# Squares of a norm kept in fp32 and added in pairs, so that half as many sum matmuls follow, in an 8-core decoder trunk

## The chip, the cores and the metric

The kernel runs on all 8 cores of one Trainium2 chip, with the same program on every core and no exchange between them. Each core works on one prompt of 2048 tokens and on 16 decode rows. The metric is the device time of the slowest core in microseconds (us).

An execution of this program can fall into a slower state: the cores of one die (0 to 3, or 4 to 7) show a lower granted TensorE clock and take some per cent longer. Only fast executions are compared here, and traces are read on cores at the full clock (about 0.98).

Names used: PE is TensorE, DVE is VectorE, ACT is ScalarE, POOL is GpSimd, SP is SyncE (which issues the stores). L700 is line 700 of the kernel; the same line has another number in every edited kernel.

## The reference, cut to what matters

```python
D_MODEL = 1024; DEPTH = 4; RMS_EPS = 1e-6

def _rmsnorm(x, g):
    xf = x.astype(jnp.float32)
    y = xf * lax.rsqrt(jnp.mean(xf * xf, axis=-1, keepdims=True) + RMS_EPS)
    return (y * g.astype(jnp.float32)).astype(x.dtype)

def _layer(x, ...):
    h = _rmsnorm(x, norm1_g)
    z = h @ w_in
    # ... gated conv branch, S5 state space branch, gated merge m ...
    x = x + m @ w_out
    h2 = _rmsnorm(x, norm2_g)
    gate, up = jnp.split(h2 @ w_gate_up, [D_FF], axis=-1)
    x = x + (jax.nn.silu(gate) * up) @ w_down
    return x, ...
# four layers, then a last _rmsnorm(x, final_g)
```

## The kernel before

The sequence is treated in two halves of 1024 tokens. The first half carries the decode rows too and is cut into three blocks of 384, 384 and 272 columns; the second has two blocks of 512. Channels lie on partitions, so the 1024 channels are eight tiles per block, and the mean over channels is a sum over partitions. A matmul with a matrix of ones makes that sum.

```python
    PP = Pool("psum", 8, lambda s: PSUM[s], reserve=3)
    SP_ = Pool("sc", NSC - 4, lambda s: SC[:, s, :], reserve=2)       # 5 shared scratch slots
    SQ = Pool("sq", 4, lambda s: SC[:, NSC - 4 + s, :], reserve=-1)   # 4 slots for the layer's parameter tables
    ...
    def norm(half, blk, l, which, src=None):
        xin = src or (lambda kt: (X[:, kt, blk.c0:blk.c0 + n], xkeys(kt, blk)))
        ps = PP.new()
        n = blk.n
        hq = lambda kt: (R if which == "fg" else H)[:, kt, blk.c0:blk.c0 + n]
        qkeys = rkeys if which == "fg" else hkeys
        for kt in range(8):
            act(lambda e, kt=kt: e.activation(out=hq(kt), in_=xin(kt)[0], func=AF.Square),
                xin(kt)[1], qkeys(kt, blk), n)
            S.pe([(lambda e, kt=kt: e.matmul(ps[:, 0:n], lhsT=ONESB[:], rhs=hq(kt), start=(kt == 0), stop=(kt == 7)),
                   qkeys(kt, blk) + [C_("ONESB")], MMN(n))], [(ps,)], FULL)
        rs = SP_.new()
        # ... Ln and Exp on ACT: rs = (mean + eps) ** -0.5 ...
        for kt in range(8):
            if which == "fg":      # the final norm
                o = SP_.new()
                # ... o = x * g * rs on DVE, then a store of o by SP ...
            else:
                # ... H[:, kt] = x * g * rs on DVE (scalar_tensor_tensor) ...
```

- The squares are bf16 and lie in H, exactly where the normalised values go afterwards. They need no slot of their own. Only the final norm ("fg") puts them into R.
- The five shared scratch slots also hold rs, the outputs of SiLU and sigmoid, and the output tiles of the final norm until their stores have landed. Four other slots belong to the layer's parameter tables. Those tables are worked out only in the first half, on DVE and POOL, and stay for the second.
- Nothing is ordered at run time. A list scheduler with its own cost model (the lines `MMN`, `ACT_`, `tt` give durations) fixes the order on every engine when the program is built, and each engine then runs its list strictly in order.

There are 45 norms per program: 27 in the first half and 18 in the second. Three of the 27, the three blocks' first norm of layer 0, are called "the start" below. The final norm of the first half and the first norm of the second half, which meet, are called "the turn".

## Time and profile before

The median is 3668.1 us over four fast executions (3666.34 to 3668.78).

| what | value | read from |
|---|---|---|
| PE busy | 3527.6 of 3684.6 us, 96% | page, busy times (core 1, the slowest in the profile) |
| DVE, ACT, POOL busy | 46%, 31%, 12% | page, busy times |
| chain of work that ended last | 91% PE | page, chain |
| PE idle before sum matmuls into H (L700) | 25.1 us | page, costliest groups |

The first fence is from the page of the kernel before: the span, the busy times, the chain by engine, and three of the costliest groups. A group line gives line, engine, operation, output<-inputs and count, then after the first bar the busy time (us) and the mean (ns) of one, then after the second bar the idle time of that engine just before these instructions and what ended most of it.

```profile
span 3684.6 us, 66888 instructions; the slowest of 8 cores (3655.5 to 3684.6 us)
PE 3527.6 (96%) x23912; PEld 1987.8 (54%) x23912; DVE 1699.6 (46%) x3049; ACT 1134.0 (31%) x2144; POOL 439.7 (12%) x639
PE 91%; DVE 3%; issue 3%; DMA 1%; ACT 1%; SPq 1%; DVEq 0%; ACTq 0%
...
L654 POOL DMA_DIRECT2D RING<-wpk x472 | 251.6, 534 | 2920.8 <-PE ps L667 2678.0
L722 DVE SCALAR_TENSOR_TENSOR H<-X,PRM,SC 128x384 bf16<-128x384 f32 (+2 forms) x304 | 190.9, 698 | 35.1 <-ACT SC L705 34.9
...
L700 PE MATMUL ps<-H,ONESB 128*128 128x384 bf16 (+2 forms) x320 | 77.6, 349 | 25.1 <-ACT H L698 25.1
```

PE is the bound. POOL spends little on arithmetic, and mostly waits for PE to free a weight slot (L654). The 320 sums into H have 25.1 us of PE idle in front of them in the whole program, nearly all of it at the start (the same view of core 6, cut to the first 262 us, has 23.5).

The second fence is from the list of cores, kernel before. Die 0 ran at a slightly lower clock in this execution, so the traces of die 1 are read.

```profile
die 0 (median of its cores): 3674.2 us, clock 0.975
die 1 (median of its cores): 3659.6 us, clock 0.981
```

The third is from the timeline of the start, kernel before, core 6. Its columns are start (us), time from first to last instruction of the row (us), engine, line, operation, count, and in brackets the idle time before it with what ended it.

```profile
30.08 2.67 ACT L698 ACTIVATE H<-X 128x272 bf16<-128x272 f32 x8 [0.27 <-DMA X<-xsT]
30.66 2.62 PE L700 MATMUL ps<-H,ONESB 128*128 128x272 bf16 x8 [2.23 <-ACT H L698]
...
32.64 12.37 DVE L722 SCALAR_TENSOR_TENSOR H<-X,PRM,SC 128x384 bf16<-128x384 f32 x15
...
33.38 0.49 ACT L703 ACTIVATE SC<-ps,CST 128x272 f32<-128x272 f32 x1 [0.63 <-PE ps L700]
```

The third block's eight squares take 2.67 us in one run, its sums follow within 0.6 us, and Ln starts at 33.38 us.

### The profile page before, as it was taken

The page shows a single profiled execution, that of the slowest core. Times are in us where ns is not written, and L with a number is a line of the kernel's source. Part 1 is how long each engine was busy: PE and PEld are TensorE (multiplying, and loading weights), DVE is VectorE, ACT ScalarE, POOL GpSimd, SP SyncE. Part 2 cuts the span into 40 slices and gives each one's busy share as a digit, 9 for nine tenths or more (in the row PEclk, how much of TensorE's full clock was granted, in tenths as well). Part 3 has the DMA queues.
Part 4 walks back from the last instruction along what each step waited for, and adds up shares of the span by engine and source line. Part 5 has one row for each costly group of instructions (what it writes and reads, how often), then busy time and mean ns, then how long its engine had stood idle before and what let it go on. Part 6 is the DMA issues. An engine that isn't in the chain of part 4 may idle for free.

```text
span 3684.6 us, 66888 instructions; the slowest of 8 cores (3655.5 to 3684.6 us)
## 1 busy us (share of the span) xinstructions
PE 3527.6 (96%) x23912; PEld 1987.8 (54%) x23912; DVE 1699.6 (46%) x3049; ACT 1134.0 (31%) x2144; POOL 439.7 (12%) x639
## 2 busy tenths in 40 slices
PE   6699999999999999999997999999999999999998
PEld 3466666666666666666653444444444444444443
DVE  8756455565545655543244532344224542255323
ACT  4442234432344323433034220332203421042202
POOL 4202210022100221000000000000000000000000
PEclk9799999999999999999998999989999999999999
DMA  7444567435564455854448444563445744474443
GB/s 159 112 80 70 113 148 144 81 70 113 145 141 86 70 113 139 185 109 75 75 83 217 77 80 70 109 144 60 79 80 106 159 69 81 69 146 79 79 70 86
DMA packets 252913, 384.11 MB, mean 104 GB/s; under 512 B 157744, under 2 KB 180912, under 8 KB 246960
## 3 DMA queue, kind: packets, MB, share of 16 engines
q0 software_dynamic: 67968, 243.30, 39.0%
q1 hardware_dynamic: 184624, 136.53, 12.6%
q8 instruction: 202, 3.31, 0.4%
q14 instruction: 119, 0.97, 0.1%
HBM read 567.06 MB, written 56.12 MB: 169 GB/s over the span
## 4 chain that ended last, share of the span: by engine, by line
PE 91%; DVE 3%; issue 3%; DMA 1%; ACT 1%; SPq 1%; DVEq 0%; ACTq 0%
PE ps L667 86%; PE ps L700 1%; PE ps L1102 1%; DMA yT<-SC 1%; DVE SC L559 1%; DVE H L722 1%; PE ps L904 1%; PE ps L1028 1%; PE ps L1075 0%; PE ps L891 0%; SPq L630 0%; DMA X<-xsT 0%; DVE X L1240 0%; DVE R L1220 0%; ACT H L698 0%
## 5 line engine op out<-in xcount | busy, mean ns | idle before, releaser
L667 PE MATMUL ps<-H,RING 128*128 128x512 bf16 (+2 forms) x12160 | 2216.8, 343 | 22.5 <-DVE H L722 9.1
L667 PEld LDWEIGHTS ps<-H,RING 128*128 128x128 bf16 x12160 | 1196.4, 99 | 980.1 <-issue 114.4
L667 PE MATMUL ps<-R,RING 128*128 128x384 bf16 (+2 forms) x6400 | 1164.8, 339 | 5.8 <-DVE X L1240 4.0
L667 PEld LDWEIGHTS ps<-R,RING 128*128 128x128 bf16 x6400 | 625.1, 98 | 505.9 <-issue 30.9
L1262 DVE TENSOR_TENSOR R<-SC,ps 128x384 bf16<-128x384 f32 (+2 forms) x440 | 255.7, 583 | 781.7 <-PE ps L667 763.8
L654 POOL DMA_DIRECT2D RING<-wpk x472 | 251.6, 534 | 2920.8 <-PE ps L667 2678.0
L1261 ACT ACTIVATE SC<-ps 128x384 f32<-128x384 f32 (+2 forms) x440 | 226.4, 515 | 1214.1 <-PE ps L667 1207.7
L1240 DVE TENSOR_TENSOR X<-X,ps 128x384 f32<-128x384 f32 (+2 forms) x480 | 270.8, 583 | 450.2 <-PE ps L667 447.1
L698 ACT ACTIVATE H<-X 128x384 bf16<-128x384 f32 (+2 forms) x304 | 156.5, 539 | 191.4 <-DVE X L1240 180.8
L722 DVE SCALAR_TENSOR_TENSOR H<-X,PRM,SC 128x384 bf16<-128x384 f32 (+2 forms) x304 | 190.9, 698 | 35.1 <-ACT SC L705 34.9
L1231 ACT ACTIVATE SC<-ps 128x384 f32<-128x384 f32 (+1 forms) x160 | 80.8, 515 | 265.5 <-PE ps L667 250.7
L1208 DVE TENSOR_TENSOR TB<-TB,ps 128x384 f32<-128x384 f32 (+2 forms) x160 | 90.4, 583 | 131.0 <-PE ps L667 114.0
L1232 DVE TENSOR_TENSOR SC<-SC,ps 128x384 f32<-128x384 f32 (+1 forms) x160 | 91.3, 582 | 87.8 <-PE ps L667 73.4
L1167 DVE TENSOR_TENSOR CIN<-ps,SC 128x384 f32<-128x384 f32 (+2 forms) x80 | 47.0, 587 | 182.7 <-ACT SC L1166 174.3
L559 DVE TENSOR_TENSOR SC<-TB 128x512 f32<-128x512 f32 (+1 forms) x160 | 120.0, 761 | 7.6 <-PE ps L904 0.6
L1153 ACT ACTIVATE TB<-ps 128x384 f32<-128x384 f32 (+1 forms) x160 | 79.6, 514 | 98.3 <-PE ps L667 97.8
L700 PE MATMUL ps<-H,ONESB 128*128 128x384 bf16 (+2 forms) x320 | 77.6, 349 | 25.1 <-ACT H L698 25.1
L1235 DVE TENSOR_TENSOR R<-TB,SC 128x384 bf16<-128x384 f32 (+1 forms) x160 | 91.6, 587 | 10.4 <-DVE SC L1232 0.9
L559 POOL TENSOR_TENSOR TB<-TB 128x512 f32<-128x512 f32 (+1 forms) x72 | 89.2, 1242 | 53.6 <-ACT H L698 32.5
L1220 DVE TENSOR_TENSOR R<-R,SC 128x384 bf16<-128x384 bf16 (+2 forms) x80 | 46.6, 588 | 74.5 <-ACT SC L1218 73.0
L895 ACT ACTIVATE TAB<-ps 128x512 bf16<-128x512 f32 x60 | 35.5, 597 | 132.0 <-PE ps L891 131.8
L1166 ACT ACTIVATE SC<-ps 128x384 f32<-128x384 f32 (+2 forms) x80 | 41.0, 514 | 95.5 <-PE ps L667 95.4
(179 smaller groups left out, 1621.2 us busy)
## 6 DMA issues: line engine op xcount, KB each, us to landing
RING<-wpk POOLq DMA_DIRECT2D x440, 512.0 KB, 7.0
TAB<-stash SPq DMA_DIRECT2D x21, 1792.0 KB, 9.4
stash<-TAB SPq DMA_DIRECT2D x15, 1792.0 KB, 7.8
R<-stash SPq DMA_DIRECT2D x7, 1792.0 KB, 14.3
RING<-wpk POOLq DMA_DIRECT2D x32, 384.0 KB, 5.9
du<-R SPq DMA_DIRECT2D x32, 256.0 KB, 9.3
UU<-du SPq DMA_DIRECT2D x32, 256.0 KB, 6.5
dy<-YY SPq DMA_DIRECT2D x32, 256.0 KB, 6.4
```

Source lines behind the costliest of these rows:

```text
L559: fn = lambda e: e.tensor_tensor(out=out(), in0=a(), in1=b(), op=op)
L654: S.dma("pool", lambda e: e.dma_start(out=t[:, 0:n], in_=wpk[l, ui, :, 0:n]), [("X",) + gate] if gate else (), [(t,)], 128 * n * 4, prio=- ...
L667: subs.append((lambda e, u=u, kw=kw, c=c, src=src, i=i: e.matmul(ps[:, 0:blk.n], lhsT=u.ap(kw, c), rhs=src(blk), start=(i == 0), stop=(i = ...
L698: act(lambda e, kt=kt: e.activation(out=hq(kt), in_=xin(kt)[0], func=AF.Square), xin(kt)[1], qkeys(kt, blk), n)
L700: S.pe([(lambda e, kt=kt: e.matmul(ps[:, 0:n], lhsT=ONESB[:], rhs=hq(kt), start=(kt == 0), stop=(kt == 7)), qkeys(kt, blk) + [C_("ONESB")] ...
L722: dve(lambda e, kt=kt, xi=xi, g=g: e.scalar_tensor_tensor(out=H[:, kt, blk.c0:blk.c0 + n], in0=xi(), scalar=g, in1=rs[:, 0:n], op0=ALU.mul ...
L1208: dve(lambda e, po=po, n=n, t_=t_, blk=blk: e.tensor_tensor(out=t_[:, blk.c0:blk.c0 + n], in0=t_[:, blk.c0:blk.c0 + n], in1=po[:, 0:n], op ...
L1232: dve(lambda e, sg=sg, po=po, n=n: e.tensor_tensor(out=sg[:, 0:n], in0=sg[:, 0:n], in1=po[:, 0:n], op=ALU.mult), [(sg,), (po,)], [(sg,)], n)
L1235: dve(lambda e, sg=sg, n=n, t_=t_, blk=blk, j=j: e.tensor_tensor(out=R[:, MT[j], blk.c0:blk.c0 + n], in0=t_[:, blk.c0:blk.c0 + n], in1=sg[ ...
L1240: dve(lambda e: e.tensor_tensor(out=X[:, j, blk.c0:blk.c0 + n], in0=X[:, j, blk.c0:blk.c0 + n], in1=ps[:, 0:n], op=ALU.add), [(ps,)] + xke ...
L1261: act(lambda e, sg=sg, pg=pg, n=n: e.activation(out=sg[:, 0:n], in_=pg[:, 0:n], func=AF.Silu), [(pg,)], [(sg,)], n, tset="silu")
L1262: dve(lambda e, sg=sg, pu=pu, n=n, blk=blk, ti=ti: e.tensor_tensor(out=R[:, ti, blk.c0:blk.c0 + n], in0=sg[:, 0:n], in1=pu[:, 0:n], op=ALU ...
```

## The change

The intent is to halve the sum matmuls on the bounding engine. Each square is written as fp32 into a scratch slot, two of them are added on an idle engine into one bf16 tile, and only that tile goes through the ones matmul. The last pair of each norm is added on DVE, the other three on POOL. The slots are the five shared ones in the first half, and the four of the parameter tables in the second half.

```diff
+NENG = "pool"
@@ in norm()
-        for kt in range(8):
-            act(lambda e, kt=kt: e.activation(out=hq(kt), in_=xin(kt)[0], func=AF.Square),
-                xin(kt)[1], qkeys(kt, blk), n)
-            S.pe([(lambda e, kt=kt: e.matmul(ps[:, 0:n], lhsT=ONESB[:], rhs=hq(kt), start=(kt == 0), stop=(kt == 7)),
-                   qkeys(kt, blk) + [C_("ONESB")], MMN(n))], [(ps,)], FULL)
+        QP = SQ if half == 1 else SP_
+        for k2 in range(4):
+            ta, tb2 = QP.new(), QP.new()
+            for t, kt in ((ta, 2 * k2), (tb2, 2 * k2 + 1)):
+                act(lambda e, kt=kt, t=t: e.activation(out=t[:, 0:n], in_=xin(kt)[0], func=AF.Square), xin(kt)[1], [(t,)], n)
+            tt(lambda k2=k2: hq(k2), lambda ta=ta: ta[:, 0:n], lambda tb2=tb2: tb2[:, 0:n], ALU.add, [(ta,), (tb2,)], qkeys(k2, blk), n,
+               eng="dve" if k2 == 3 else NENG)
+            S.pe([(lambda e, k2=k2: e.matmul(ps[:, 0:n], lhsT=ONESB[:], rhs=hq(k2), start=(k2 == 0), stop=(k2 == 3)),
+                   qkeys(k2, blk) + [C_("ONESB")], MMN(n))], [(ps,)], FULL)
```

## The prediction

> **What bounds the kernel.** TensorE. The page gives PE 96% busy (3527.6 of 3684.6 us), DVE 46%, ACT 31%, POOL 12%; the chain of work that ended last is 91% PE, 86% of it the projection line L667. In the timeline of the second half, 236 projections of 512 columns take 51.10 us, 216.5 ns each, back to back. So matmuls removed from the middle of the program are worth their pitch (start to next start), and delays elsewhere cost only where PE has no other work.
>
> **What is removed.** 45 norms (27 on blocks of 384/384/272 columns, 18 on 512) make 360 sum matmuls (L700); 180 go. Their busy time of 77.6 us for 320 counts pipeline latency (349 ns each), so I use the pitch: median 163, 116 and 216 ns for 384, 272 and 512 columns by the trace's start times. 72 x 0.163 + 36 x 0.116 + 72 x 0.216 = 31.5 us, 0.86% of the span. The sums take 1% of the chain, which agrees.
>
> **What is added.** 180 adds: 135 on POOL, 45 (the last pair of each norm) on DVE. By the groups by shape, a POOL add of two fp32 inputs takes 1306 ns at 512 columns (1360 with bf16 out) and 733 at 256; interpolated, about 1.02 us at 384 and 0.77 at 272. That is about 150 us on POOL (440 becomes about 590). DVE adds about 27 us (0.69 us at 512). The 360 squares stay on ACT, now fp32 out, same time.
>
> **What moves.** The latency of a norm's last sum grows by one DVE add plus a semaphore, about 0.8 us; the first three adds are mostly hidden, because two X blocks come every 3.4 us (eight matmuls each) and an add takes 1.3. The squares leave H/R and use scratch slots: five shared ones in the first half, four idle ones in the second. The Trainium skill, "SBUF — State Buffer", section "Who interferes with whom", says that a DVE instruction with two SBUF inputs contends with a GpSimd instruction that reads SBUF, the second one blocking. L722 (X and SC) is such an instruction; its median is 617 ns and its longest 1617, which fits. So some normalising DVE instructions wait about 1 us; DVE has slack. POOL also issues the weights (L654), but sits idle 2678 us there waiting for PE to free ring slots, so an add of 1.3 us ahead of an issue is absorbed by the prefetch.
>
> **On the critical path.** Nearly all 31.5 us in the middle. Against it: the start (PE's projections begin at 32.5 us, behind loads, norms and table work on a crowded DVE and POOL): +2 to 5 us; the end, where sum, Ln, Exp and scaling are exposed: +0.8 us; the turn between the halves, where output tiles compete for the same five slots: 0 to 5 us. The order is made by a list scheduler, so the whole order shifts, by a few us either way.
>
> **Prediction.** 3642 us (-0.7%), 8 in 10 between 3628 and 3660. Faster by over 2%: 0.02; within 2%: 0.95; slower by over 2%: 0.03.
>
> **What would show it.** L700 180 times at unchanged pitch, PE busy down about 40 us (by the page's count); POOL busy up about 150 us; DVE up 27 us plus blocked time; PE's wait before L700 on POOL or DVE under 15 us in total; projections starting 2 to 5 us later; weight issues still waiting for PE.
>
> **What would make it wrong.** PE, in fixed order, stalling at sums that wait for POOL adds held up by DVE or by a weight issue ahead of them (135 x 0.3 us would eat the gain); scratch slots in the first half holding back SiLU or squares; table work slowed by blocking in the first half; a luckier order gaining more.

## The result, and the profile after

The fast executions of the kernel after took 3683.36, 3685.95 and 3682.78 us; those of the kernel before 3666.34 to 3668.78. The ratio of fast runs is 1.0044 (95% interval 1.0025 to 1.0064): slower by 0.4%. A ratio is the mean time of one kernel's fast runs over that of the other's fast runs in the same rounds, so it is not quite the ratio of the medians quoted.

The profiled execution was a slow one: the next fence is from the list of cores, kernel after.

```profile
die 0 (median of its cores): 3676.1 us, clock 0.981
die 1 (median of its cores): 3753.6 us, clock 0.958
```

Die 0 was undisturbed and is read for times. The page is that of core 4 on the slow die, so its PE times are long; its counts and its DVE and POOL times still serve.

```profile
span 3758.0 us, 66802 instructions; the slowest of 8 cores (3663.6 to 3758.0 us)
PE 3546.8 (94%) x23564; PEld 1985.8 (53%) x23732; DVE 1765.5 (47%) x3094; ACT 1158.4 (31%) x2166; POOL 586.7 (16%) x774
PE 83%; DVE 6%; issue 4%; DMA 3%; ACT 2%; SPq 1%; POOL 1%; DVEq 0%; ACTq 0%; POOLq 0%
...
L655 POOL DMA_DIRECT2D RING<-wpk x472 | 254.0, 539 | 2591.2 <-PE ps L668 2411.8
L727 DVE SCALAR_TENSOR_TENSOR H<-X,PRM,SC 128x384 bf16<-128x384 f32 (+2 forms) x304 | 213.0, 768 | 25.5 <-PE ps L668 12.4
...
L560 POOL TENSOR_TENSOR H<-SC 128x384 bf16<-128x384 f32 (+2 forms) x120 | 130.1, 1086 | 225.1 <-ACT SC L702 192.5
L705 PE MATMUL ps<-H,ONESB 128*128 128x384 bf16 (+2 forms) x155 | 47.3, 346 | 44.0 <-POOL H L560 18.0
```

The matmuls did go: 23912 weight loads became 23732, which is 180 fewer. (Matmul records are missing for 168 of the 23732, so weight loads are counted.) The chain shows what was bought with them: PE holds 83% of it instead of 91%, and DVE, DMA, ACT and POOL hold more. PE's idle time before sums into H rose from 25.1 to 44.0 us, though there are half as many. Core 2 of the undisturbed die says the same: 82% of the chain, 44.3 us.

To see where the time went, the program is cut at three landmarks that every trace has: the end of DVE's first residual addition (into X) of layer 0, of layer 3, and of the second half's layer 0. Times are means over undisturbed cores of the profiled execution. "PE work" is the sum of matmul columns divided by 2.4 per ns. The Trainium skill, "Trainium Kernel Development and Optimization", section "NeuronCore Architecture", gives TensorE 2.4 GHz; the trace agrees to 1.5%: 216.5 ns from start to start against 213.3 for 512 columns. What a stretch grew by beyond its PE work is called additional PE idle time. It is a remainder and not a measured wait; it also holds any change of the granted clock.

| us | start | three layers of first half | last layer and turn | rest of second half | whole |
|---|---|---|---|---|---|
| before | 262.4 | 1380.4 | 459.7 | 1556.8 | 3659.3 |
| after | 279.5 | 1384.3 | 464.1 | 1546.0 | 3673.9 |
| difference | +17.1 | +3.9 | +4.4 | -10.8 | +14.5 |
| of it PE work | -1.7 | -10.4 | -5.2 | -13.7 | -31.0 |
| of it PE idle | +18.8 | +14.3 | +9.6 | +2.9 | +45.5 |

So 31.0 us of PE work were saved, against 31.5 predicted, and 45.5 us of new idle time ate them. The second half came out about as predicted. The largest single item is the start.

The waits of PE in the same traces account for most of the remainder. All gaps between PE's instructions grew by 16.5, 11.0, 6.4 and 4.8 us in the four stretches. In front of the sums alone PE waited 23.0 us at the start, nothing in the next two stretches and 4.0 in the rest before the change; after it 29.7, 7.3, 15.5 and 10.5. That is 27.0 us in all before and 63.0 after.

The next fence is from the timeline of the start, kernel after, core 2, to be held against that of the kernel before.

```profile
30.62 0.75 ACT L702 ACTIVATE SC<-X 128x272 f32<-128x272 f32 x2 [1.88 <-POOL H L560]
...
38.07 1.11 DVE L560 TENSOR_TENSOR H<-SC 128x384 bf16<-128x384 f32 x1
...
42.17 10.60 DVE L727 SCALAR_TENSOR_TENSOR H<-X,PRM,SC 128x384 bf16<-128x384 f32 x8
...
42.96 0.75 ACT L702 ACTIVATE SC<-X 128x272 f32<-128x272 f32 x2
...
52.69 1.50 DVE L560 TENSOR_TENSOR H<-SC 128x272 bf16<-128x272 f32 x1
54.87 0.49 ACT L708 ACTIVATE SC<-ps,CST 128x272 f32<-128x272 f32 x1 [1.05 <-PE ps L705]
```

The third block's squares no longer run as eight in a row. The first pair waits for a POOL addition (1.88 us), and the last pair comes only at 42.96 us, after the second block's last addition on DVE (38.07) and the third block's first ones have freed slots. Then the third block's own last addition stands in DVE's list behind eight normalising operations of the second block that take 10.60 us, 1.33 us each. Its Ln starts at 54.87 instead of 33.38 us. The last normalising operation of the start ends at 61.2 us instead of about 45. PE's first projection comes no later than before (31.1 against 33.1 us); the delay builds up behind it.

### The profile page after: what moved, and what is told of

The parts are those of the page before. It is cut to its first block, busy times and chain, and to the rows that moved or that the text cites. A ratio compares the mean times of both kernels' runs of the same rounds, so it can differ in the third digit from the quotient of the medians.

```text
span 3758.0 us, 66802 instructions; the slowest of 8 cores (3663.6 to 3758.0 us)
## 1 busy us (share of the span) xinstructions
PE 3546.8 (94%) x23564; PEld 1985.8 (53%) x23732; DVE 1765.5 (47%) x3094; ACT 1158.4 (31%) x2166; POOL 586.7 (16%) x774
## 3 DMA queue, kind: packets, MB, share of 16 engines
q14 instruction: 124, 1.02, 0.1%
## 4 chain that ended last, share of the span: by engine, by line
PE 83%; DVE 6%; issue 4%; DMA 3%; ACT 2%; SPq 1%; POOL 1%; DVEq 0%; ACTq 0%; POOLq 0%
PE ps L668 79%; DVE H L727 3%; DMA dy<-YY 1%; PE ps L1107 1%; DMA yT<-SC 1%; ACT SC L702 1%; PE ps L705 1%; PE ps L1033 1%; PE ps L909 1%; DVE R L1225 1%; DVE X L1245 1%; PE ps L1080 0%; POOL H L560 0%; ACT SC L1223 0%; DVE SC L560 0%
## 5 line engine op out<-in xcount | busy, mean ns | idle before, releaser
L668 PE MATMUL ps<-H,RING 128*128 128x384 bf16 (+2 forms) x12041 | 2239.2, 345 | 36.8 <-DVE H L727 17.0
L668 PE MATMUL ps<-R,RING 128*128 128x384 bf16 (+2 forms) x6356 | 1184.4, 344 | 18.3 <-DVE X L1245 8.6
L655 POOL DMA_DIRECT2D RING<-wpk x472 | 254.0, 539 | 2591.2 <-PE ps L668 2411.8
L1266 ACT ACTIVATE SC<-ps 128x384 f32<-128x384 f32 (+2 forms) x440 | 226.1, 515 | 1185.8 <-PE ps L668 1167.1
L702 ACT ACTIVATE SC<-X 128x384 f32<-128x384 f32 (+2 forms) x344 | 177.5, 538 | 233.5 <-DVE X L1245 199.9
L727 DVE SCALAR_TENSOR_TENSOR H<-X,PRM,SC 128x384 bf16<-128x384 f32 (+2 forms) x304 | 213.0, 768 | 25.5 <-PE ps L668 12.4
L560 POOL TENSOR_TENSOR H<-SC 128x384 bf16<-128x384 f32 (+2 forms) x120 | 130.1, 1086 | 225.1 <-ACT SC L702 192.5
L705 PE MATMUL ps<-H,ONESB 128*128 128x384 bf16 (+2 forms) x155 | 47.3, 346 | 44.0 <-POOL H L560 18.0
## 6 DMA issues: line engine op xcount, KB each, us to landing
R<-stash SPq DMA_DIRECT2D x7, 1792.0 KB, 14.5
```

Of the source, the lines that this page charges most:

```text
L560: fn = lambda e: e.tensor_tensor(out=out(), in0=a(), in1=b(), op=op)
L655: S.dma("pool", lambda e: e.dma_start(out=t[:, 0:n], in_=wpk[l, ui, :, 0:n]), [("X",) + gate] if gate else (), [(t,)], 128 * n * 4, prio=- ...
L668: subs.append((lambda e, u=u, kw=kw, c=c, src=src, i=i: e.matmul(ps[:, 0:blk.n], lhsT=u.ap(kw, c), rhs=src(blk), start=(i == 0), stop=(i = ...
L702: act(lambda e, kt=kt, t=t: e.activation(out=t[:, 0:n], in_=xin(kt)[0], func=AF.Square), xin(kt)[1], [(t,)], n)
L705: S.pe([(lambda e, k2=k2: e.matmul(ps[:, 0:n], lhsT=ONESB[:], rhs=hq(k2), start=(k2 == 0), stop=(k2 == 3)), qkeys(k2, blk) + [C_("ONESB")] ...
L727: dve(lambda e, kt=kt, xi=xi, g=g: e.scalar_tensor_tensor(out=H[:, kt, blk.c0:blk.c0 + n], in0=xi(), scalar=g, in1=rs[:, 0:n], op0=ALU.mul ...
```

## The experiments

### The theories

- **A**: the loss is the start, as just read. Two parts can be told apart: **A1**, the squares wait for scratch slots, and **A2**, the addition itself comes late, in particular the one on DVE. **F** is A2's later, sharper form: the last addition waits in DVE's queue behind normalising operations that POOL slows.
- **C**: in the middle of the program PE stalls at sums that wait for additions on POOL.
- **E**: at the turn the squares wait for scratch slots that hold output tiles whose stores have not landed.
- Rivals: the sums were never worth 31 us of PE; or the build-time order simply came out unlucky.

The texts quoted as "expected" use these letters; where they use another word for a theory, they name one of these or one of the rivals.

For every kernel the differences from the kernel before are given by the four stretches of the table above, and the change of PE work where it matters. Kernels of one group of runs share the runs of the kernel before. Its stretches come from its one profile, while its fast runs in later groups, on other chips, were mostly up to 4 us shorter: a stretch difference of a few us is not a finding. All results were correct except r3.

### r1: the old norm at the start, the new one elsewhere

```diff
+        if half == 0 and l == 0 and which == "n1":   # the three norms of the start
+            ... loop of the kernel before ...
+        else:
             ... loop of the kernel after ...
```

> The change everywhere except in the three norms that open the program, which keep eight bf16 squares and eight sums. Theory A (the opening norms hold up layer 0: squares wait for two of five scratch slots, which come free only after in-order adds on POOL and DVE that stand among the parameter work): the mark 'first residual add of layer 0' goes back from about 280 to about 263 us, and the total falls about 15 us below the changed kernel, to about 3658 to 3668 us. Theory B (the loss is PE stalling at sums throughout): the total stays within 5 us of the changed kernel, 3678 to 3688 us.

Measured: fast runs 3665.65 and 3661.47 us, ratio 0.9989 (0.9967 to 1.0010). Stretches +0.2, +1.7, +4.9, -11.5: -4.7 in all, with PE work down 29.2. The first residual addition of layer 0 came at 262.6 us, as in the kernel before (262.4). The 17 us of the start go away with its three norms, so A holds. But PE work is down 29.2 and only 4.7 arrive: something else takes the rest in the middle and at the turn.

### r2: the new norm at the start, the old one elsewhere

The condition of r1 with its branches exchanged.

> The mirror: only the three opening norms are changed, all others are as before. Theory A: first residual add of layer 0 at about 278 to 282 us against 262, and the total 12 to 17 us above the kernel before (3680 to 3685). Theory B: total within 4 us of before.

Measured: 3685.27, 3686.38 and 3685.81 us, ratio 1.0050 (1.0029 to 1.0072). Stretches +18.7, +0.9, +1.0, -2.5. Three norms of 45 make the whole slowdown on their own, and the delay is not made up later. The -2.5 in a second half that has not changed shows how far such a difference can be trusted.

### r3: half the sums and no additions (wrong result)

```diff
-        for kt in range(8):
+        for kt in range(0, 8, 2):
...
-            ... start=(kt == 0), stop=(kt == 7)
+            ... start=(kt == 0), stop=(kt == 6)
...
-            ... func=AF.Ln, bias=CST[:, 0:1], scale=1.0 / D
+            ... func=AF.Ln, bias=CST[:, 0:1], scale=2.0 / D
```

Only every second channel tile enters the mean, so the result is off (relative error 0.057).

> Wrong result on purpose: the kernel before with only the four even squares and four sums per norm, no adds, scale doubled. It takes away the 180 sums (31.5 us of pitch) and adds nothing. If the matmul price is right and nothing else limits, the total is 3668 - 30 = 3632 to 3642 us. If list-schedule luck or other waits eat PE savings anyway, it is above 3650.

Measured: fast runs 3622.73 and 3616.59 us, ratio 0.9869 (0.9848 to 0.9890), below the expected range. Stretches -0.3, -15.8, -0.4, -31.1: -47.6, with PE work down 31.0. Removing the sums is worth at least their PE work, so the rival "not worth it" falls. The run also drops 180 squares on ACT, so it isn't a clean price: the 16.6 us beyond the PE work may be theirs, or the order's. At the start and the turn it gained nothing, -0.3 and -0.4 us for 1.7 and 5.2 us of PE work: there the end of the stretch does not hang on PE's work, so these 6.9 us of the price were hardly to be had.

### r4: r1 with all additions on DVE

```diff
-NENG = "pool"
+NENG = "dve"
```

> As r1, but all adds on DVE (about 0.69 us at 512 columns instead of 1.3 on POOL). Theory C (the in-order POOL queue and its long add make PE stall at the sums in the middle, about 13 us in the first half): faster than r1 by 5 to 15 us. Rival D (the stall is the extra link itself, scratch slots and DVE's own queue): within 4 us of r1, or slower because DVE's own adds delay the residual adds.

Measured: 3662.54 to 3670.20 us, ratio 0.9996 (0.9980 to 1.0012). The total is that of r1, and the total alone would have said that POOL is innocent. The stretches say otherwise: -0.5, -7.4, +19.0, -16.9. The middle and the second half gained 14.5 over r1 and the turn lost 14.1. (By the letter of the expectation the total met rival D.)

First the middle. The next three fences are from the one-line view of the sum matmuls in the three layers of the first half: kernel before (core 6), r1 (core 2), r4 (core 2). The first row gives count and duration in ns (minimum/median/maximum); the rows below give the idle time just before the line's instructions, in us and how often, by what ended it. The line has weight loads too (PEld, shown for r1), and the view adds both engines up: the rows "issue" are PEld's and no waiting of PE; those that name POOL or DVE are PE's.

```profile
L700 PE MATMUL ps<-H,ONESB x144: 278/326/327, 271.6 to 1478.6; 128*128 128x384 bf16 x96, 128*128 128x272 bf16 x48
its engine sat idle before it (us, times) until:
  issue: 0.8, 4
```

```profile
L712 PEld LDWEIGHTS ps<-H,ONESB x72: 95/98/98, 269.8 to 1472.7; 128*128 128x128 bf16 x72
L712 PE MATMUL ps<-H,ONESB x72: 276/326/326, 270.0 to 1472.7; 128*128 128x384 bf16 x48, 128*128 128x272 bf16 x24
its engine sat idle before it (us, times) until:
  issue: 13.5, 18
  POOL H L560: 4.8, 6
  DVE H L560: 2.9, 7
```

```profile
L712 PE MATMUL ps<-H,ONESB x72: 276/326/326, 269.5 to 1468.8; 128*128 128x384 bf16 x48, 128*128 128x272 bf16 x24
its engine sat idle before it (us, times) until:
  issue: 1.6, 6
```

With the additions on POOL, PE stands 7.7 us before its sums in these layers (4.8 for POOL + 2.9 for DVE); before the change it did not wait there, and with all additions on DVE it doesn't. The stretch gained 9.1 us by the move, about as much. C holds for the middle, though r10 below shows another cure.

Then the turn. The timeline of the turn in r4, core 2:

```profile
1927.64 0.62 DVE L724 SCALAR_TENSOR_TENSOR SC<-X,PRM,SC 128x384 f32<-128x384 f32 x1 [13.06 <-DMA yT<-SC]
...
1933.20 0.94 ACT L709 ACTIVATE SC<-X 128x384 f32<-128x384 f32 x2 [8.47 <-DVE SC L724]
...
1934.53 0.48 PE L712 MATMUL ps<-R,ONESB 128*128 128x384 bf16 x1 [8.01 <-DVE R L560]
```

An output tile of the final norm waits 13.06 us for a store (yT<-SC) to free its slot, the next squares wait 8.47 us behind it, and PE waits 8.01 us for their sum. Over the whole turn PE waited 25.7 us before sums in r4 (mean of the cores), 14.5 in r1 and not at all before the change. This suggested E.

### r7: r4, with the old norm at the turn too

```diff
-        if half == 0 and l == 0 and which == "n1":
+        if half == 0 and (l == 0 and which == "n1" or which == "fg") or src is not None:
```

> Pairs in fp32 scratch with all adds on DVE, but the old norm at the start and at the turn of the halves (the staged norms and the first half's final norm). r4, which has the turn changed, had gained 8 us by the fourth layer and then lost 19 at the turn. Theory E (at the turn, squares wait for scratch slots that output tiles hold while their stores queue): this run keeps the 8 us and gains on in the second half: 3638 to 3650 us. If the turn's loss is schedule luck: 3655 us or more.

Measured: 3633.57 to 3640.04 us, median 3636.51, ratio 0.9922 (0.9905 to 0.9940). Stretches -1.1, -7.5, -1.3, -22.3: -32.2, with PE work down 25.8. The total is just below the expected range. The turn went from +19.0 to -1.3, so the new norm at the turn was the cause. This run removes its additions together with its slots, so it doesn't yet show that the slots were it. r8 and r10, which add at the turn without slots for the squares, say how much: PE's wait before sums there is 9.8 us in r8 against 25.7 in r4 (both on DVE), and 11.6 in r10 against 14.5 in r1 (three of four on POOL). So E holds for about 16 us of r4's wait, and for only about 3 of the change's own; some 10 come with the additions themselves.

### r5: the start with squares in H instead of slots

The pairs can be added in place: square both into H in bf16, add the second onto the first, sum the first. No slot is needed. The price is that squares are rounded to bf16 before the addition, as the kernel before rounded them anyway. Only the start uses this loop; all other norms are the old ones, so it is to be compared with r2.

```diff
+            for k2 in range(4):
+                for kt in (2 * k2, 2 * k2 + 1):
+                    act(... activation(out=hq(kt), in_=xin(kt)[0], func=AF.Square) ...)
+                tt(hq(2 * k2), hq(2 * k2), hq(2 * k2 + 1), ALU.add, ..., eng="dve" if k2 == 3 else NENG)
+                S.pe([... matmul(ps, lhsT=ONESB, rhs=hq(2 * k2), start=(k2 == 0), stop=(k2 == 3)) ...])
```

> Only the three opening norms are changed, as in r2 (which was 17 us over the kernel before), but their squares stay in H as bf16 and are added there in place, by the same engines as in the change; no scratch slot is used. Theory A1 (the opening loss comes from waiting for shared scratch slots): first residual add of layer 0 at 262 to 268 us instead of 281, total within 6 us of before. Theory A2 (it comes from the adds themselves standing in the in-order queues of POOL and DVE among the parameter work): first residual add at 275 us or later, total 10 us or more over before.

Measured: 3670.35 to 3675.81 us, ratio 1.0021 (1.0004 to 1.0038). The first residual addition came at 273.7 us, against 281.1 in r2 and 262.4 before. Slots are 7.4 us of the 18.7, so neither A1 nor A2 is the whole, and both expectations were missed. The timeline of the start in r5, core 4, shows what is left:

```profile
31.20 2.60 POOL L560 TENSOR_TENSOR H<-H 128x272 bf16<-128x272 bf16 x3 [0.66 <-ACT H L707]
...
36.20 11.99 DVE L732 SCALAR_TENSOR_TENSOR H<-X,PRM,SC 128x384 bf16<-128x384 f32 x11
48.11 1.35 DVE L560 TENSOR_TENSOR H<-H 128x272 bf16<-128x272 bf16 x1
```

POOL's three additions of the third block end at 33.8 us. The fourth, on DVE, runs at 48.11 us, behind eleven normalising operations that take 1.09 us each. That is F.

### r9: r5 with the start's last addition on POOL too

```diff
-                tt(..., eng="dve" if k2 == 3 else NENG)
+                tt(..., eng=NENG)
```

> As r5 (opening norms only, squares in H, first residual add of layer 0 at 274 us instead of 262), but the last pair of each norm is added on POOL as well, so that no add stands in DVE's queue. In r5 the third norm's last add had its inputs by 33 us and ran on DVE at 48.1 us, behind eleven normalising instructions that took 1.09 us each. Theory F (DVE's in-order queue is the rest of the opening loss): first residual add at 262 to 267 us. Rival G (the adds' own time and POOL's queue): it stays at 271 us or later.

Measured: the two runs counted as fast (3694.83 and 3699.44 us) had single cores at clock 0.974, and no ratio could be given. The cores at full clock have 3662.9 us on average, +3.6 against the kernel before. The first residual addition came at 268.2 us, 5.5 earlier than r5: between what F (262 to 267) and its rival G (271 or later) expected. So of the 18.7 us, about 7.4 are slots, 5.5 DVE's queue, and 5.8 remain with the additions themselves in whatever order results. The split comes from first-half marks on undisturbed cores, not from the totals, and is good to some 2 us: r6 below opens as r5 does and has +8.9 there, where r5 has +11.3.

### r6: every norm in H, additions where the change has them

The loop of r5 in all 45 norms.

> The whole change, with only the place of the squares undone (bf16 in H or R, pairs added in place, same engines). A1: loses neither the 17 us at the start nor the 8 us at the turn of the halves: 3650 to 3660 us. A2: 3675 us or more. In both the stalls of PE at sums that wait for POOL in the middle stay (first-half step 'wo last' about +2 us a layer).

Measured: 3646.74 to 3653.17 us, median 3648.26, ratio 0.9956 (0.9939 to 0.9974). Stretches +8.9, -8.8, +0.7, -19.8: -18.9. The total is what A1 expected or a little better, but the start kept about half of its loss. It is 35 us better than the change itself, with the same PE work and the same engines: doing without slots (and adding bf16 instead of fp32, which comes with it) makes the difference between a slower and a faster kernel.

### r8: old norm at the start, pairs in H on DVE elsewhere

This puts the findings together: nothing new at the start, no slots, no POOL.

```diff
+        if half == 0 and l == 0 and which == "n1":
+            ... loop of the kernel before ...
+        else:
+            ... loop of r5, NENG = "dve" ...
```

> Old norm at the start only; everywhere else pairs of bf16 squares added in place in H or R by DVE. No scratch slots, no POOL adds. Theories A1, C and E together: 3632 to 3648 us, that is most of the 31.5 us. If the extra DVE link itself costs PE stalls: 3655 us or more.

Measured: 3612.86 to 3616.03 us, median 3614.01, ratio 0.9862 (0.9843 to 0.9882). This is 18 us below the expected range, and it beats both kernels, by 1.4% and by about 1.9%. Stretches -0.9, -30.3, +4.2, -25.5: -52.5. The first lines of its page:

```profile
span 3611.2 us, 66445 instructions; the slowest of 8 cores (3600.4 to 3611.2 us)
PE 3457.3 (96%) x23744; PEld 1961.3 (54%) x23744; DVE 1737.0 (48%) x3217; ACT 1143.9 (32%) x2156; POOL 438.4 (12%) x639
...
L732 DVE SCALAR_TENSOR_TENSOR H<-X,PRM,SC 128x384 bf16<-128x384 f32 (+2 forms) x304 | 177.5, 654 | 28.3 <-ACT SC L715 27.8
```

POOL is back at 438 us, and DVE at 1737 has less to do than in the kernel after (1765.5), although it makes 168 additions instead of 45. The additions are cheaper, but 168 of them still take about 62 us against 31; what pays for them is mostly the normalising group, 177.5 us instead of 213.0 now that POOL makes no additions and the order is another. The groups by shape give the price of one addition: kernel after (core 2), r4 (core 2), r8 (core 3), all for 512 columns.

```profile
L560 POOL TENSOR_TENSOR H<-SC 128x512 bf16<-128x512 f32 x48 | 61.0, 1275 | 97.5 <-ACT SC L702 77.9 <-PE ps L668 11.3 <-DVE X L1245 8.2
```

```profile
L560 DVE TENSOR_TENSOR H<-SC 128x512 bf16<-128x512 f32 x64 | 43.7, 689 | 23.3 <-ACT SC L709 22.9
```

```profile
L560 DVE TENSOR_TENSOR H<-H 128x512 bf16<-128x512 bf16 x64 | 26.4, 421 | 19.3 <-ACT H L707 19.3
```

One addition costs 1275 ns on POOL, 689 on DVE from fp32 and 421 on DVE from bf16. The Trainium skill, "VectorE: DVE Perf Modes", section "The perf-mode tier table", gives tensor_tensor twice the speed for bf16 in SBUF (1224 against 2293 ns at 2048 elements). Here the ratio is 1.64 at 512. With 436 and 293 ns at 272 columns in the same lists, each further column costs 1.05 ns from fp32 and 0.53 from bf16, which is the factor of two; an estimated 0.15 us of either addition is fixed. The skill's "GPSIMD Engine Reference", section "Elementwise — side-by-side cycle accounting", has about 2.6 cycles per element at 1.2 GHz for POOL: an estimate of 1109 ns for 512 elements from that page, plus fixed cost, against 1275 measured.

r8 gained 23.3 us more than its PE work. About 20 of these lie in the three layers of the first half. There the trace shows an effect that has nothing to do with sums. It is read from traces; no run tests it alone. Two timelines, kernel before (core 6) and r8 (core 3), at the third block's normalising in one layer:

```profile
762.46 5.46 POOL L559 TENSOR_TENSOR TB<-TB 128x512 f32<-128x512 f32 x4
764.26 7.88 DVE L722 SCALAR_TENSOR_TENSOR H<-X,PRM,SC 128x272 bf16<-128x272 f32 x8
...
768.37 0.28 PE L667 MATMUL ps<-H,RING 128*128 128x272 bf16 x1 [0.95 <-DVE H L722]
```

```profile
748.67 3.39 DVE L732 SCALAR_TENSOR_TENSOR H<-X,PRM,SC 128x272 bf16<-128x272 f32 x8 [0.37 <-ACT SC L715]
...
756.45 1.57 POOL L560 TENSOR_TENSOR TB<-TB 128x512 f32<-128x512 f32 x1
```

In the kernel before, the eight operations run beside POOL's work on parameter tables and take 7.88 us, with a median of 1.30 us and up to 1.54 us instead of 0.49 alone, and PE waits for three of them (3.1 us). In r8 the order has them before POOL's work, and they take 3.39 us. The step from a layer's first residual addition (of w_out) to its first of w_down is about 9 us shorter in each of the three layers (158.0 to 149.1 us in this one), of which 1.7 is saved PE work. A wait costs more here than it lasts: the trace of the kernel before gives PE half its clock from 772.4 to 775.8 us, right behind these three waits, and the matmuls of 272 columns then start every 227 ns instead of every 116; r8's trace has no such window in this step. In the three layers PE's gaps fell by 10.1 us in r8 and the time lost to half clock by 7.3, which is 17.4 of the 20. The Trainium skill, "SBUF — State Buffer", section "Who interferes with whom", says that a DVE instruction with two SBUF inputs contends with a GpSimd instruction that reads SBUF. The trace agrees: while both run, DVE's and POOL's instructions alternate one for one, and the five slow ones of DVE (1.30 to 1.54 us) each end 0.3 us after the POOL instruction beside them.

### r10: r8 with three of four additions on POOL

```diff
-NENG = "dve"
+NENG = "pool"
```

> Fills the square of place by engine, all with the old norm at the start: scratch and POOL r1 (ratio 0.9989), scratch and DVE r4 (0.9996), H and DVE r8 (0.9862), and here H with the change's own engines. If the place is what matters: 3622 to 3635 us (r6 less its 9 us at the start is about 3638). If it needs both, 3640 us or more.

Measured: one fast run of 3664.22 us with cores 0 and 1 at clock 0.973, and no ratio. The cores at full clock have 3628.2 us on average and 3640.4 at most, so the total can't decide between its two expectations. Stretches -0.7, -9.1, +1.9, -23.3: -31.2, with PE work down 29.2. PE's wait before sums in the three layers is 2.4 us (mean of the cores), against 7.8 with slots (r1) and none in r8. So C has two parts: slots deepen the wait for POOL, and some of it stays without them. Of the 12.1 us that r1 lost in this stretch beyond its PE work, taking away the slots (here) recovers 10.8 and taking away POOL (r4) 9.1: either is enough. The turn of +4.9 in r1 is here +1.9 and that of r4, +19.0, is +4.2 in r8: the slots' share at the turn is small with POOL and large with DVE.

### r11 and r12: the same work in another order

The scheduler's model of an ACT instruction was changed from 0.17 to 0.18 us fixed cost, in the kernel before (r11) and in r8 (r12). No instruction changes, only the order.

```diff
-ACT_ = lambda n: 0.17 + n * 0.833e-3
+ACT_ = lambda n: 0.18 + n * 0.833e-3
```

> The kernel before with one constant of the scheduler's cost model moved (ScalarE's fixed cost 0.17 to 0.18 us): same instructions, another order. It measures the luck of the order. If it moves by 3 us or less, differences of 10 us between variants are the variants' own; if it moves by 10 us or more, they are not.

> r8 with the same moved constant. r8 gained 52 us where 31.5 were priced; about 21 us of that sat in three first-half stretches, where the kernel before had PE waiting for normalising instructions that ran beside POOL's parameter work. If that part is luck of the order, this run lies 5 to 25 us above r8 (3620 to 3640); if not, within 4 us of 3614.

Measured: r11 3662.44 to 3666.65 us, ratio 0.9977 (0.9925 to 1.0029), stretches +0.3, +2.4, -1.0, -7.6. r12 3617.18 to 3624.04 us, median 3619.2, ratio 0.9855 (0.9811 to 0.9898), stretches -0.3, -29.6, +5.8, -24.0. So order alone is worth several us: r11 moved the second half by 7.6 us with no work changed. r12 lies 5 us above r8, just outside the 4 us that its expectation allowed for no luck. But r8's three steps of -9 us in the middle stayed in r12, so they are not a lucky draw of one order.

### What could not be tried

Putting all additions on DVE at the start as well (with slots or in H) and changing the model's semaphore delay (0.07 to 0.09) made the scheduler itself stop without an order: the pools of slots deadlocked at build time. Slots of its own for the start did not fit into SBUF. None of these went to the chip.

## Why the prediction was right or wrong

- **The price of the sums was right.** 31.5 us were predicted from start-to-start times, and the PE work fell by 31.0; that is a count of columns, and r3 (-47.6 us) shows that it was to be had. PE's busy time, which counts the tails of matmuls too, fell by 25 us and not by the 40 predicted (3502.7 to 3477.4, on undisturbed cores whose records are complete). The group's own mean (349 ns each) would have doubled the price.
- **The added work was right.** POOL rose by 147 us (439.7 to 586.7), about 150 predicted. Additions on POOL took 1275, 1010 and 858 ns for 512, 384 and 272 columns, against 1.31 to 1.36, 1.02 and 0.77 us. DVE rose by 66 us; 22 of them are the normalising group growing from 190.9 to 213.0, the "blocked time" that the prediction named. The weight loads' issues still wait for PE (2411.8 of 2591.2 us), as predicted.
- **The step that failed first: "the start [...] +2 to 5 us".** It measured +17.1 (18.8 beyond PE work), shown by r1 and r2. The prediction saw a crowded DVE and POOL and priced only the addition's own duration. What it left out is position: a slot is freed by an addition that stands in an in-order list (about 7.4 us, r5), and the last addition stands behind normalising operations at 1.1 to 1.3 us each (5.5 us, r9). In the kernel after this happens twice: the second block's last addition (38.07 us) stands behind the first block's normalising, and the third's (52.69) behind the second's.
- **The step that failed second: "Nearly all 31.5 us in the middle", with stalls before sums "under 15 us in total".** The three layers of the first half had 14.3 us of additional idle time and the last layer with the turn 9.6. PE's wait before sums outside the start rose from 4.0 to 33.3 us: 7.3 in the three layers, 15.5 in the last layer and the turn, 10.5 in the rest. The claim that the first three additions "are mostly hidden" failed in the first half; r4 shows it by moving them to DVE (7.8 us of wait in r1, none in r4), and r10 by taking away the slots (2.4). And 6.9 of the 31.0 us lie at the start and the turn, where r3 gained nothing by dropping them. In the second half, where POOL has no table work and the slots are four of their own, additional idle was only 2.9 us, less than the order's own spread.
- **The end (+0.8) and the second half** were not contradicted. **The turn (0 to 5)** measured +4.4 in time for the last layer and turn together, so its size was inside, partly by luck: 5.2 us of saved work are in it, and most of PE's wait there is not the slots that the prediction named (14.5 us in r1, 11.6 without slots in r10). In r4 the slots do cost about 16.
- **The failed terms together.** With the measured idle terms (18.8 at the start, 14.3 in three layers, 9.6 in the last layer and the turn, 2.9 in the rest) against 31.0 us of work saved, the sum is +14.6 us instead of the predicted -26: 3668.1 + 14.6 = 3682.7, against about 3684 measured. This is bookkeeping and no test, since the idle terms are themselves remainders of the measured time.
- **"What would make it wrong" named the right things.** Scratch slots, PE in fixed order stalling at POOL additions, and blocking were all listed, but as risks without a size. The range of 3628 to 3660 had no room for them. The chance of 0.95 for "within 2%" was right.

What stays open: why the order with the normalising before POOL's work arises only when both H and DVE are used (r8, r12) and not in r4, r7 or r10. The second-half gains of r1 (-11.5), r4 (-16.9), r10 (-23.3) and r8 (-25.5) can't be fully separated from the order's own spread, which r11 puts at 7.6 us. The last 5.8 us of the start were not split, nor the 10 us or so that PE waits at the turn without any slot. The slot and queue shares come from single differences of marks, and the slot share of 7.4 us also contains the cheaper addition of bf16 inputs.

## What to carry to other kernels

When work is moved from the bounding engine to idle ones, its price is less in the durations than in what it must wait for: count which slot it needs, who frees that slot, and what stands ahead in that engine's in-order list, and look separately at the start and at every turn, where nothing hides the wait. If the result can lie where its successor will be written (here, squares in H), no slot is needed and the small tile may be cheaper too. Read a change by stretches, since r4's unchanged total hid a gain of about 25 us and a loss of 19. And when a view adds up several engines, see whose idle time it is before it is counted as the bound's.

## What the Trainium skill lacked or had wrong

- "SBUF — State Buffer", section "Who interferes with whom", has the contention of DVE and GpSimd but no figure for two-input operations against each other. Here a DVE scalar_tensor_tensor of 272 columns took 1.30 to 1.54 us beside POOL additions and multiplications, 0.49 alone, each ending 0.3 us after the POOL instruction beside it.
- "GPSIMD Engine Reference", section "Elementwise — side-by-side cycle accounting", has no figure for bf16 inputs of a two-input addition. At 512 columns it took 1161 ns from bf16 (r6) and 1275 from fp32, so bf16 gains POOL only 9%, where it gains DVE 39%.
- No page read speaks of scratch slots as a cost when squares, outputs or stores share them between engines that run in order. Here that was worth about 7.4 us at the start (r2 against r5) and about 15 at the turn (r4 against r8), each with the cheaper bf16 addition in it.
